# Delta net on one Trainium2 core: key norm applied to the rows of the system, query norm folded into the output norm, decay sums spread by DMA

## The chip, the cores and the metric

The kernel runs on one core of one Trainium2 chip, as one program. The metric is the device time of one launch in microseconds, the median of several runs. A core has five engines with queues of their own: TensorE (PE, with its weight loads PEld), VectorE (DVE), ScalarE (ACT), GpSimd (POOL) and SyncE (SP). All DMAs of this kernel are issued from SP's queue, in order. Each engine works through its own queue in order and waits on semaphores for the others.

## The reference

One step of a decoder layer for 1024 prompt tokens and 8 x 8 sample tokens, 1088 columns in all: a half-step SwiGLU, a mixer of two branches with a gated sum, a second half-step SwiGLU, each between RMS norms. Branch A is sliding-window attention; branch B is a short convolution and a gated delta net of 4 heads with key and value width 128. The change is within branch B:

```python
qb = l2_normalize(qb.reshape(bsz, t, B_HEADS, B_KEY_DIM)) * (B_KEY_DIM ** -0.5)
kb = l2_normalize(kb.reshape(bsz, t, B_HEADS, B_KEY_DIM))
...
gc = jnp.cumsum(g, axis=-1)
...
decay = jnp.exp(jnp.where(incl, gc[..., :, None] - gc[..., None, :], -jnp.inf))
k_beta = k * beta[..., None]
m = jnp.where(strict, jnp.einsum('...id,...jd->...ij', k_beta, k) * decay, 0.0)
a = m + jnp.eye(c, dtype=m.dtype)
...
qk = jnp.einsum('...id,...jd->...ij', q, k) * decay
q_dec = q * jnp.exp(gc)[..., None]
...
ob = rms_norm(ob, dn_out_norm) * jax.nn.silu(zb)
```

with `l2_normalize(x) = x * rsqrt(sum(x * x) + EPS)` over the 128 features of a token and head. The system `a` is solved for its right sides, a scan over chunks carries the state, and the output is normed per token and head.

## The kernel before

Tokens lie along the free dimension, features along the 128 partitions. The 1088 tokens are cut into the column blocks of 384, 384 and 320. Weights are loaded by SP in 256 KB pieces, split into two float32r parts (a high part by ACT, L111, a rest by DVE, L112), and each product is done as three (L138 to L140). The program has a first FFN, the projections for keys, values and queries of branch A with the attention, the units of the convolution (`qkv`), of z and of the gates (`ga`), four delta heads, then the branch products, the output product and the second FFN.

The framework that records the program orders the instructions on each engine. Where a delta head's small products wait, it puts products of a conv, z or gate unit (written to the tiles `pa`, three of them in PSUM) in between. DVE empties each `pa` tile (L957, L1018, L1031). The text below calls these products fillers.

`delta_head(h, A, ps)` works on eight tiles of 128 x 1088 (the set `HA` for heads 0 and 2, `YA` for 1 and 3; the profile shows all of them as `s`) and on a PSUM ring of two tiles, `ph` for heads 0 and 2, `py` for 1 and 3. Its steps:

- `l2` for q and for k (L1049, L1050). `colsum_rsqrt` squares the tile on ACT (L998), sums over the partitions by three products with a tile of ones (L1001, 512 + 512 + 64 columns), scales (L1002), takes the reciprocal root on ACT (L1003, with a table load) and refines it by a Newton step (L144 to L146). Then DVE scales the tile (L1008).
- For two groups of four chunks of 128 tokens: the running sums of g are spread over all partitions by a product of a broadcast column of g with a triangle (L1060, into `pr`), k against q (L1063), the decay (L1066, L1074, L1075), the product with it (L1077), the decay's transpose (L1080), k against k (L1083) and the system's matrix M with beta as a factor on its rows (L1087). The 64 sample tokens get the same at L1099 to L1114.
- Diagonal 32 x 32 blocks go through DRAM (`bd`) and are inverted by forward substitution on DVE (L1143, L1149), while k and v are transposed (L1135, L1202, L1203).
- The inverse is completed by products (L1174 to L1198) with the scales beta and beta exp(gc) (L1165, L1166).
- The scan over eight chunks (L1217 to L1236), then the sample tokens (L1246 to L1270).
- The output norm: `colsum_rsqrt` again, on the output tile QK (L1276), the scale (L1277), the product with z on POOL (L1278) and the store to `obd`.

The sums gc themselves, one column per chunk and head, are made once before the attention (L759 to L778).

Of the kernel before, what the change touches and what calls it, by code (L numbers as in the profile page):

```python
# [7 lines left out]
F32 = mybir.dt.float32  # L8
# [27 lines left out]
def body(ctx: ExitStack, tc: tile.TileContext, d):  # L36
# [25 lines left out]
    gd = dp.tile([16, P, NT], F32, tag="gd", name="gd")  # L62

# [716 lines left out]

    vtok = YA[6]
# [215 lines left out]
    def colsum_rsqrt(src, sq, ve, rr, tmp, scale, ps):  # L997
        nc.scalar.activation(sq, src, AF.Square)  # L998
        for a, b in ((0, 512), (512, 1024), (1024, NT)):
            pq = ps()  # L1000
            nc.tensor.matmul(pq[:, : b - a], ones, sq[:, a:b], start=True, stop=True)  # L1001
            nc.scalar.activation(ve[:, a:b], pq[:, : b - a], AF.Identity, scale=scale, bias=epsc)  # L1002
        nc.scalar.activation(rr, ve, AF.Abs_reciprocal_sqrt)  # L1003
        newton(rr, ve, tmp)

    def l2(x, A, l2s, ps):
        colsum_rsqrt(x, A[4], A[3], A[5], A[4], 0.25, ps)
        nc.vector.scalar_tensor_tensor(out=x, in0=x, scalar=-0.25 * l2s, in1=A[5], op0=ALU.mult, op1=ALU.mult)  # L1008
# [31 lines left out]
    def delta_head(h, A, ps):  # L1040
        q, k, v, M, L, U, QK, R = A
        ar = R[:, :NPR].rearrange("p (i c) -> p i c", c=P)
        mq = s2b.tile([P, 2 * NSM], F32, tag="mq", name=f"mq{h}", bufs=2)

# [4 lines left out]
        l2(q, A, P ** -0.5, ps)  # L1049
        l2(k, A, 1.0, ps)  # L1050
        def wide(t, c0):
            return t[:, c0 * P : c0 * P + 512]

        D, E = R[:, 0:512], R[:, 512:1024]
        for c0 in (0, 4):
            pr, pq = ps(), ps()
            for i in range(4):
                w, cs, ix = tile_of(c0 + i)
                ps_i = slice(i * P, i * P + P)
                nc.tensor.matmul(pr[:, ps_i], tk["g"][:, ix : ix + 1].to_broadcast([P, P]), cst[:, C_TRI : C_TRI + P], start=True, stop=True)  # L1060
            for i in range(4):
                w, cs, ix = tile_of(c0 + i)
                nc.tensor.matmul(pq[:, i * P : i * P + P], k[:, cs], q[:, cs], start=True, stop=True)  # L1063
            for i in range(4):
# [3 lines left out]
                    in0=pr[:, i * P : i * P + P],  # L1068
# [5 lines left out]
            nc.scalar.activation(E, pr, AF.Exp)  # L1074
# [6 lines left out]
            for i in range(4):  # L1081
                w, cs, ix = tile_of(c0 + i)
                nc.tensor.matmul(pk[:, i * P : i * P + P], k[:, cs], k[:, cs], start=True, stop=True)  # L1083
            nc.scalar.copy(D, pt)
            for i in range(4):
# [4 lines left out]
                    scalar=tk["beta"][:, ix : ix + 1],  # L1090
# [416 lines left out]
```

## Time and profile before

| what | value |
|---|---|
| median of 3 runs | 2460.74 us (2459.77 to 2460.8) |
| the profiled execution's own time | 2454.17 us |
| its span, first to last instruction | 2452.4 us |
| granted TensorE clock, mean | 0.991 |
| DMA traffic | 257.98 MB, 105 GB/s over the span |

The profile is of one execution, and its durations are compared with that execution's time. A page line such as `PE 2396.3 (98%) x14654` gives busy time, share of the span and instructions. A group's row has line, engine, operation, output and inputs, shape and count, then busy time and the mean of one in ns, then the idle time of the engine ahead of the group and what ended it. A wait's row reads: engine, output and line that waited, what it waited for, the time in all, how often, and the longest.

### The profile page before, as it was taken

The numbers are of one execution on the slowest core, as the hardware profiler recorded it, in microseconds if no ns is written. First come the engines' busy times: TensorE is split into PE (matmuls) and PEld (weight loads), VectorE is DVE, ScalarE is ACT, GpSimd is POOL, SyncE is SP. The second block draws the span as 40 slices with busy tenths as digits, with TensorE's granted clock in tenths as the row PEclk, the third lists the DMA queues.
The fourth block names the chain that finished last, engine by engine and source line by source line (L and its number), as shares of the span: only waits on it lengthen the run. The fifth ranks groups of instructions, "written<-read, shape, count | busy, mean of one in ns | idle before, by whom it ended". The sixth has DMA issues, their size and how long they took to land.

```text
span 2452.4 us, 39218 instructions
## 1 busy us (share of the span) xinstructions
PE 2396.3 (98%) x14654; PEld 2307.2 (94%) x14654; DVE 1752.0 (71%) x3550; ACT 1146.2 (47%) x2326; POOL 48.6 (2%) x36
## 2 busy tenths in 40 slices
PE   8999999999999999999999999999999999999997
PEld 7999999999998988798898889999999999999997
DVE  8887657757788577698796646655997576676677
ACT  7644423324465377644655333255754333233344
POOL 0000000000000000000101000000000000000000
PEclk9999999999999999999999999999999999999998
DMA  7332212213454301222222345435523122122453
GB/s 269 125 112 86 74 48 86 70 52 112 155 175 142 105 29 45 77 65 73 71 68 73 99 143 158 142 129 184 182 93 97 48 82 78 45 85 80 152 164 133
DMA packets 159759, 257.98 MB, mean 105 GB/s; under 512 B 34800, under 2 KB 65968, under 8 KB 159560
## 3 DMA queue, kind: packets, MB, share of 16 engines
q1 hardware_dynamic: 159568, 255.47, 32.4%
q8 instruction: 115, 1.88, 0.3%
q14 instruction: 76, 0.62, 0.1%
HBM read 219.43 MB, written 36.96 MB: 105 GB/s over the span
## 4 chain that ended last, share of the span: by engine, by line
PE 43%; DVE 6%; DMA 2%; ACT 1%; issue 1%; SPq 0%; DVEq 0%; ACTq 0%
PE pa L139 6%; PE pa L140 6%; PE pa L138 6%; PE pa L462 4%; PE pa L463 4%; PE pa L464 4%; PE py L344 2%; PE py L345 2%; PE ph L345 2%; PE ph L344 2%; PE ph L343 2%; PE py L343 2%; DMA q_c_a<-in_up_dram 1%; DVE s L1149 1%; DVE s L1143 1%
## 5 line engine op out<-in xcount | busy, mean ns | idle before, releaser
L463 PE MATMUL pa<-cl,h_c_s 128*128 128x384 f32 x704 | 236.4, 336 | 4.7 <-DVE cl L272 4.7
L462 PE MATMUL pa<-ch,h_c_s 128*128 128x384 f32 x704 | 237.4, 337 | 2.0 <-DVE t L468 1.4
L464 PE MATMUL pa<-ch,l_c_s 128*128 128x384 f32 x704 | 236.2, 336 | 0.0
L468 DVE TENSOR_TENSOR t<-pa,t 128x384 f32<-128x384 f32 x308 | 170.3, 554 | 83.6 <-PE pa L464 83.1
L462 PE MATMUL pa<-ch,h_c_a 128*128 128x384 f32 x528 | 176.8, 335 | 0.1
L464 PE MATMUL pa<-ch,l_c_a 128*128 128x384 f32 x528 | 176.6, 334 | 0.0
L463 PE MATMUL pa<-cl,h_c_a 128*128 128x384 f32 x528 | 176.5, 334 | 0.0
L111 ACT CAST h_c_a<-r_c_a 128x512 fp32r<-128x512 f32 x132 | 81.8, 619 | 129.8 <-PE pa L463 110.9
L462 PEld LDWEIGHTS pa<-ch,h_c_s 128*128 128x128 f32 x704 | 132.8, 189 | 5.6 <-DVE t L468 5.2
L463 PEld LDWEIGHTS pa<-cl,h_c_s 128*128 128x128 f32 x704 | 133.0, 189 | 4.9 <-DVE cl L272 4.9
L464 PEld LDWEIGHTS pa<-ch,l_c_s 128*128 128x128 f32 x704 | 132.9, 189 | 0.0
L111 ACT CAST h_c_s<-q_c_s 128x512 fp32r<-128x512 f32 x132 | 82.0, 621 | 107.1 <-PE pa L463 96.3
L139 PE MATMUL pa<-xbl,h_ga 128*128 128x384 f32 (+1 forms) x384 | 129.3, 337 | 0.0
L138 PE MATMUL pa<-xbh,h_ga 128*128 128x384 f32 (+1 forms) x384 | 128.7, 335 | 0.0
L140 PE MATMUL pa<-xbh,l_ga 128*128 128x384 f32 (+1 forms) x384 | 128.4, 334 | 0.0
L462 PEld LDWEIGHTS pa<-ch,h_c_a 128*128 128x128 f32 x528 | 99.1, 188 | 0.8 <-DVE t L468 0.6
L463 PEld LDWEIGHTS pa<-cl,h_c_a 128*128 128x128 f32 x528 | 99.1, 188 | 0.0
L464 PEld LDWEIGHTS pa<-ch,l_c_a 128*128 128x128 f32 x528 | 99.1, 188 | 0.0
L138 PE MATMUL pa<-xbh,h_qkv 128*128 128x384 f32 (+1 forms) x288 | 96.7, 336 | 0.0
L139 PE MATMUL pa<-xbl,h_qkv 128*128 128x384 f32 (+1 forms) x288 | 96.6, 335 | 0.0
L140 PE MATMUL pa<-xbh,l_qkv 128*128 128x384 f32 (+1 forms) x288 | 96.3, 334 | 0.0
L111 ACT CAST h_c_s<-r_c_s 128x512 fp32r<-128x512 f32 x44 | 27.4, 623 | 146.4 <-PE pa L463 130.6
(603 smaller groups left out, 7438.4 us busy)
## 6 DMA issues: line engine op xcount, KB each, us to landing
r_c_a<-in_up_dram SPq DMA_DIRECT2D x132, 256.0 KB
q_c_a<-in_up_dram SPq DMA_DIRECT2D x44, 256.0 KB
q_ub<-in_up_dram SPq DMA_DIRECT2D x44, 256.0 KB
r_ub<-in_up_dram SPq DMA_DIRECT2D x44, 256.0 KB
r_ua<-in_up_dram SPq DMA_DIRECT2D x42, 256.0 KB
q_ua<-in_up_dram SPq DMA_DIRECT2D x42, 256.0 KB
r_da<-in_dn_dram SPq DMA_DIRECT2D x40, 256.0 KB
q_da<-in_dn_dram SPq DMA_DIRECT2D x40, 256.0 KB
```

The costliest lines, as they stand in the source:

```text
L111: nc.scalar.copy(hi, full)
L138: nc.tensor.matmul(ps[:, :n], hi[:, j, :], at(xh, k), start=first, stop=False)
L139: nc.tensor.matmul(ps[:, :n], hi[:, j, :], at(xl, k), start=False, stop=False)
L140: mm = nc.tensor.matmul(ps[:, :n], lo[:, j, :], at(xh, k), start=False, stop=last)
L343: nc.tensor.matmul(ps[:, :n], hi[:, i, :], hh, start=i == 0, stop=False)
L344: nc.tensor.matmul(ps[:, :n], hi[:, i, :], hl, start=False, stop=False)
L345: nc.tensor.matmul(ps[:, :n], lo[:, i, :], hh, start=False, stop=i == len(hs) - 1)
L462: nc.tensor.matmul(ps, wh[:, k, :], xh[:, k, :], start=k == 0, stop=False)
L463: nc.tensor.matmul(ps, wh[:, k, :], xl[:, k, :], start=False, stop=False)
L464: nc.tensor.matmul(ps, wl[:, k, :], xh[:, k, :], start=False, stop=k == 3)
L468: nc.vector.tensor_tensor(out=out, in0=ps, in1=other, op=ALU.add)
L1143: nc.vector.tensor_tensor(out=tv, in0=Md[:, j + 1 :, j : j + 1].to_broadcast([34, m, j + 1]), in1=Ld[:, j : j + 1, 0 : j + 1].to_broadcast ...
```

## The change

Queries and keys are no longer scaled before they are multiplied. `colsum_rsqrt` and `l2` are gone.

- Keys: k is transposed at the head's start (nine transposes, which stood in the middle of the head before). ACT squares the transposed tiles, DVE reduces them to one sum per token, nine columns for a head, and a reciprocal root with a Newton step runs on these 128 x 9 values. The factors enter where beta stood: its square in the rows of M (`br2`) and in the scale of the key side (`bgr`), the factor itself on the value side (`bhr`). The old k stays as `kT_` and its tile is later reused as L; the transposed k takes the tile that was L, and the sample part has a small tile `k8`.
- Queries: the square of q, scaled with the norm's epsilon, is stored to DRAM (`sqd`) at the head's start and read back at the end, where DVE adds it to the square of the output, so that the sum over partitions under the output norm contains it. The output norm is the only one left that sums over partitions by products with ones.
- Decay sums: gc is transposed once, its 36 rows are stored to DRAM (`gcd`), and each head reads its row spread over the 128 partitions into QK by one DMA. The products L1060 and L1099 are gone; the decay and its exponents read QK in SBUF.

```diff
@@ -62,0 +63,2 @@
+    gcd = dp.tile([4, 9, P], F32, tag="gcd", name="gcd")
+    sqd = dp.tile([4, P, NT], F32, tag="sqd", name="sqd")
@@ -778,0 +781,8 @@
+    psc = pb()
+    nc.tensor.transpose(psc[:36, :P], tk["gc"], ident)
+    gct = s2b.tile([36, P], F32, tag="gct", name="gct")
+    nc.vector.tensor_copy(gct, psc[:36, :P])
+    for c in range(9):
+        nc.sync.dma_start(gcd[:, c, :], gct[4 * c : 4 * c + 4, :])
@@ -997,12 +1007,2 @@
-    def colsum_rsqrt(src, sq, ve, rr, tmp, scale, ps):
-        nc.scalar.activation(sq, src, AF.Square)
-        for a, b in ((0, 512), (512, 1024), (1024, NT)):
-            pq = ps()
-            nc.tensor.matmul(pq[:, : b - a], ones, sq[:, a:b], start=True, stop=True)
-            nc.scalar.activation(ve[:, a:b], pq[:, : b - a], AF.Identity, scale=scale, bias=epsc)
-        nc.scalar.activation(rr, ve, AF.Abs_reciprocal_sqrt)
-        newton(rr, ve, tmp)
-    def l2(x, A, l2s, ps):
-        colsum_rsqrt(x, A[4], A[3], A[5], A[4], 0.25, ps)
-        nc.vector.scalar_tensor_tensor(out=x, in0=x, scalar=-0.25 * l2s, in1=A[5], op0=ALU.mult, op1=ALU.mult)
+    eps4 = s2b.tile([P, 1], F32, tag="eps4", name="eps4")
+    nc.vector.memset(eps4, 4.0 * P * EPS * EPS)
@@ -1041 +1041,6 @@
-        q, k, v, M, L, U, QK, R = A
+        q, kT_, v, M, k, U, QK, R = A
+        L = kT_
@@ -1043,0 +1049 @@
+        k8 = s2b.tile([NSM, P], F32, tag="k8", name=f"k8{h}", bufs=2)
@@ -1049,2 +1054,0 @@
-        l2(q, A, P ** -0.5, ps)
-        l2(k, A, 1.0, ps)
@@ -1053,0 +1058,3 @@
+        nc.sync.dma_start(QK, gcd[h].rearrange("c t -> (c t)")[0:NT].unsqueeze(0).to_broadcast([P, NT]))
+        nk = s2b.tile([P, 5, 9], F32, tag="nk", name=f"nk{h}", bufs=2)
+        ss, rho, rho2, t9, bgr = (nk[:, i, :] for i in range(5))
@@ -1054,0 +1062,29 @@
+        nc.vector.memset(ss, 1.0)
+        for c0 in (0, 4, 8):
+            n = 4 if c0 < 8 else 1
+            w = P if c0 < 8 else NSM
+            pt = ps()
+            for i in range(n):
+                nc.tensor.transpose(pt[:w, i * P : i * P + P], kT_[:, (c0 + i) * P : (c0 + i) * P + w], ident)
+            nc.scalar.copy(wide(k, c0) if c0 < 8 else k8, pt[:w, : n * P])
+            nc.scalar.activation(M[:w, : n * P], pt[:w, : n * P], AF.Square)
+            nc.vector.tensor_reduce(
+                out=ss[:w, c0 : c0 + n], in_=M[:w, : n * P].rearrange("p (i c) -> p i c", c=P), op=ALU.add, axis=AX.X
+            )
+        nc.vector.tensor_scalar_add(ss, ss, 4.0 * EPS)
+        nc.scalar.activation(rho, ss, AF.Abs_reciprocal_sqrt)
+        newton(rho, ss, t9)
+        nc.vector.tensor_scalar_mul(rho, rho, -0.5)
+        nc.vector.tensor_tensor(out=rho2, in0=rho, in1=rho, op=ALU.mult)
+        def mine(nm):
+            return v94(tk[nm])[:, :, h]
+        bgr, bhr, br2 = t9, ss, bgr
+        nc.vector.tensor_tensor(out=bgr, in0=mine("bg"), in1=rho2, op=ALU.mult)
+        nc.vector.tensor_tensor(out=bhr, in0=mine("bh"), in1=rho, op=ALU.mult)
+        nc.vector.tensor_tensor(out=br2, in0=mine("beta"), in1=rho2, op=ALU.mult)
+        nc.scalar.activation(U, q, AF.Square, scale=P * EPS ** 0.5)
+        nc.sync.dma_start(sqd[h], U)
@@ -1056 +1092 @@
-            pr, pq = ps(), ps()
+            pq = ps()
@@ -1059,5 +1095 @@
-                ps_i = slice(i * P, i * P + P)
-                nc.tensor.matmul(pr[:, ps_i], tk["g"][:, ix : ix + 1].to_broadcast([P, P]), cst[:, C_TRI : C_TRI + P], start=True, stop=True)
-            for i in range(4):
-                w, cs, ix = tile_of(c0 + i)
-                nc.tensor.matmul(pq[:, i * P : i * P + P], k[:, cs], q[:, cs], start=True, stop=True)
+                nc.tensor.matmul(pq[:, i * P : i * P + P], kT_[:, cs], q[:, cs], start=True, stop=True)
@@ -1068 +1100 @@
-                    in0=pr[:, i * P : i * P + P],
+                    in0=QK[:, cs],
@@ -1074 +1106 @@
-            nc.scalar.activation(E, pr, AF.Exp)
+            nc.scalar.activation(E, wide(QK, c0), AF.Exp)
@@ -1083 +1115 @@
-                nc.tensor.matmul(pk[:, i * P : i * P + P], k[:, cs], k[:, cs], start=True, stop=True)
+                nc.tensor.matmul(pk[:, i * P : i * P + P], kT_[:, cs], kT_[:, cs], start=True, stop=True)
@@ -1090 +1122 @@
-                    scalar=tk["beta"][:, ix : ix + 1],
+                    scalar=br2[:, c0 + i : c0 + i + 1],
@@ -1097 +1129 @@
-            tri, neg = cst[:w, C_TRIS : C_TRIS + w], cst[:w, C_NEGS : C_NEGS + w]
+            neg = cst[:w, C_NEGS : C_NEGS + w]
@@ -1099,3 +1131,2 @@
-            nc.tensor.matmul(p[:, 0:w], tk["g"][:w, ix : ix + 1].to_broadcast([w, P]), tri, start=True, stop=True)
-            nc.tensor.matmul(p[:w, 128 : 128 + w], k[:, cs], k[:, cs], start=True, stop=True)
-            nc.tensor.matmul(p[:w, 256 : 256 + w], k[:, cs], q[:, cs], start=True, stop=True)
+            nc.tensor.matmul(p[:w, 128 : 128 + w], kT_[:, cs], kT_[:, cs], start=True, stop=True)
+            nc.tensor.matmul(p[:w, 256 : 256 + w], kT_[:, cs], q[:, cs], start=True, stop=True)
@@ -1104 +1135 @@
-                out=Ds, in0=p[:w, 0:w], scalar=tk["gc"][:w, ix : ix + 1], in1=neg, op0=ALU.subtract, op1=ALU.add
+                out=Ds, in0=QK[:w, cs], scalar=tk["gc"][:w, ix : ix + 1], in1=neg, op0=ALU.subtract, op1=ALU.add
@@ -1108 +1139 @@
-            nc.scalar.activation(eR, p[:, 0:w], AF.Exp)
+            nc.scalar.activation(eR, QK[:, cs], AF.Exp)
@@ -1115 +1146 @@
-                out=M[:w, cs], in0=p[:w, 128 : 128 + w], scalar=tk["beta"][:w, ix : ix + 1], in1=DT, op0=ALU.mult, op1=ALU.mult
+                out=M[:w, cs], in0=p[:w, 128 : 128 + w], scalar=br2[:w, c : c + 1], in1=DT, op0=ALU.mult, op1=ALU.mult
@@ -1132,5 +1163,4 @@
-            for t in (k, v):
-                p = ps()
-                for i in range(4):
-                    nc.tensor.transpose(p[:, i * P : i * P + P], t[:, (c0 + i) * P : (c0 + i + 1) * P], ident)
-                nc.scalar.copy(wide(t, c0), p)
+            p = ps()
+            for i in range(4):
+                nc.tensor.transpose(p[:, i * P : i * P + P], v[:, (c0 + i) * P : (c0 + i + 1) * P], ident)
+            nc.scalar.copy(wide(v, c0), p)
@@ -1165,2 +1195,2 @@
-            nc.vector.tensor_scalar_mul(Ub, U[:w, cs], tk["bg"][:w, ix : ix + 1])
-            nc.scalar.mul(U[:w, cs], U[:w, cs], tk["bh"][:w, ix : ix + 1])
+            nc.vector.tensor_scalar_mul(Ub, U[:w, cs], bgr[:w, c : c + 1])
+            nc.scalar.mul(U[:w, cs], U[:w, cs], bhr[:w, c : c + 1])
@@ -1202 +1231,0 @@
-        nc.tensor.transpose(p[:w, 0:128], k[:, cs], ident)
@@ -1204 +1233 @@
-        nc.scalar.copy(ar[:w, 6:8, :], p[:w, 0:256].rearrange("p (i c) -> p i c", c=P))
+        nc.scalar.copy(ar[:w, 7, :], p[:w, 128:256])
@@ -1208 +1237 @@
-        nc.tensor.matmul(p5[:, :w], ar[:w, 6, :], Ub, start=True, stop=True)
+        nc.tensor.matmul(p5[:, :w], k8, Ub, start=True, stop=True)
@@ -1269 +1298 @@
-            nc.tensor.matmul(p6, ar[:NSM, 6, :], vm, start=True, stop=True)
+            nc.tensor.matmul(p6, k8, vm, start=True, stop=True)
@@ -1276 +1305,9 @@
-        colsum_rsqrt(QK, q, k, v, M, 1.0 / P, ps)
+        nc.sync.dma_start(v, sqd[h])
+        nc.scalar.activation(q, QK, AF.Square)
+        nc.vector.tensor_tensor(out=q, in0=q, in1=v, op=ALU.add)
+        for a, b in ((0, 512), (512, 1024), (1024, NT)):
+            pq = ps()
+            nc.tensor.matmul(pq[:, : b - a], ones, q[:, a:b], start=True, stop=True)
+            nc.scalar.activation(k[:, a:b], pq[:, : b - a], AF.Identity, scale=1.0 / P, bias=eps4)
+        nc.scalar.activation(v, k, AF.Abs_reciprocal_sqrt)
+        newton(v, k, M)
```

The changed instructions stand in a different order on the engines. Three places follow. In the rows `s_...` are a head's wide tiles, `pa_...` the fillers' output, `eye_72` holds the identity and the ones; line numbers of the first fence of a pair are those of the kernel before, those of the second of the changed kernel.

TensorE at the start of the third head (its ring is `ph`, while the second head's scan L1217 to L1235 runs on `py`), before: the products with ones for k's norm (L1001) and behind them the first spread of the sums of g (L1060).

```order
L1001 MATMUL ph_12686<-s_8312,eye_72 128x512
L1001 MATMUL ph_12689<-s_8312,eye_72 128x512
L1224 MATMUL py_11724<-s_8307,s_8303 128x128
L1235 MATMUL py_11731<-s_8306,s_8307 128x128
L1001 MATMUL ph_12692<-s_8312,eye_72 128x64
L140 MATMUL pa_13257<-xbh_1_8036,l_ga_1_13225 128x384
L138 MATMUL pa_13257<-xbh_1_8036,h_ga_1_13224 128x384
L1060 MATMUL ph_12700<-cst,tk_g 128x128
L1217 MATMUL py_11735<-s_8304,s_8301 128x128
L1219 MATMUL py_11735<-s_8307,s_8305 128x128
L1234 MATMUL py_11742<-s_8302,s_8307 128x128
L1060 MATMUL ph_12700<-cst,tk_g 128x128 x3
```

The same place in the changed kernel: the last transposes of k (L1068) and k against q (L1095), with the second head's inverse (L1204 and on, before L1174 and on) between them.

```order
L140 MATMUL pa_13159<-xbh_0_8245,h_ga_0_13091 128x320
L1068 MATMUL ph_12669<-eye_72,s_8311 128x128 x2
L1068 MATMUL ph_12677<-eye_72,s_8311 64x128
L141 MATMUL pa_13159<-xbl_0_8247,h_ga_0_13091 128x320
L1204 MATMUL py_11605<-s_8303,s_8307 128x128 x4
L142 MATMUL pa_13159<-xbh_0_8245,l_ga_0_13092 128x320
L1095 MATMUL ph_12694<-s_8310,s_8311 128x128 x4
L1208 MATMUL py_11611<-s_8309,s_8305 128x128 x4
```

The products with ones and the spread of g are gone, transposes of k stand at the start of the head, and k against q follows them with no spread of g ahead of it. The third head now starts beside the second head's inverse and not beside its scan.

TensorE at the output norm of the second head, before: the two products for the new sample states (L1269), one filler, and the products with ones (L1001), with transposes of the next head (L1135) between them.

```order
L1269 MATMUL py_11821<-s_8303,s_8307 128x512
L1269 MATMUL py_11825<-s_8303,s_8307 128x512
L140 MATMUL pa_13327<-xbh_0_7313,l_qkv_0_13318 128x384
L1001 MATMUL py_11831<-s_8302,eye_72 128x512
L1135 MATMUL ph_12786<-eye_72,s_8309 128x128
L1001 MATMUL py_11834<-s_8302,eye_72 128x512
L1001 MATMUL py_11837<-s_8302,eye_72 128x64
```

The same place in the changed kernel, from the second product for the sample states (L1298) to the first with ones (L1310):

```order
L1298 MATMUL py_11810<-s_8302,k_11402 128x512
L141 MATMUL pa_13258<-xbl_1_8248,h_ga_1_13196 128x320
L142 MATMUL pa_13258<-xbh_1_8246,l_ga_1_13197 128x320
L140 MATMUL pa_13299<-xbh_0_7315,h_qkv_0_13289 128x384
L141 MATMUL pa_13299<-xbl_0_7317,h_qkv_0_13289 128x384
L142 MATMUL pa_13299<-xbh_0_7315,l_qkv_0_13290 128x384
L140 MATMUL pa_13299<-xbh_0_7315,h_qkv_0_13289 128x384
L1310 MATMUL py_11818<-s_8304,eye_72 128x512
```

Six fillers stand there now, and three more stand between the two L1298.

DVE at the same output norm in the changed kernel: the sum that closes the output (L1285), the masks (L1291), the two additions to the sample states (L1299) and the new addition of sqd (L1307), with the release of a filler's tile (L1031).

```order
L1285 TENSOR_TENSOR s_8308<-py_11798,s_8309 128x64
L1291 TENSOR_TENSOR s_8302<-s_8309,cst 64x512
L1299 TENSOR_TENSOR s_8305<-s_8305,py_11806 128x512
L1307 TENSOR_TENSOR s_8304<-s_8304,s_8306 128x1088
L1031 SCALAR_TENSOR_TENSOR t_1142_13283<-pa_13258,r_8267 128x320
L114 TENSOR_TENSOR l_ga_1_14143<-r_ga_1_14140,h_ga_1_14142 128x512
L1299 TENSOR_TENSOR s_8305<-s_8305,py_11810 128x512
```

The new addition stands ahead of a filler's release and of the second L1299.

## The prediction

> **What bounds the kernel now.** I read the head of the page first, then the windows of the stage that the change touches, then the waits of TensorE there, and last single stretches of its timeline.
>
> ```profile
> span 2452.4 us, 39218 instructions
> PE 2396.3 (98%) x14654; PEld 2307.2 (94%) x14654; DVE 1752.0 (71%) x3550; ACT 1146.2 (47%) x2326; POOL 48.6 (2%) x36
> 900.00:1460.00 560.00, 544.14 (x3522) 483.97 (x3523) 413.66 (x1090) 301.97 (x670) 48.42 (x32) 0.99 0.24 74
> 1460.00:1640.00 180.00, 180.00 (x1110) 179.39 (x1109) 110.16 (x206) 67.75 (x139) 0.00 (x0) 1.00 0.48 155
> ```
>
> In a window's row the columns are its bounds, its length, the busy time of PE, weight loads, DVE, ACT and POOL, the granted clock, the DMA share and GB/s. TensorE is busy 98% of the span. The four delta heads run from about 900 to 1460 us, and there TensorE is busy 544 of 560 us, because the products of the conv, z and gate units are woven between the heads' own small products. After the last head comes a stretch of 180 us without a gap, gate products and then the branch products. So no head's chain sets the end: the length of the stage is **the sum of TensorE's work, plus its gaps, plus what a lowered clock costs**. A microsecond of TensorE work taken out of the stage shortens the kernel by a microsecond, as long as no new gap takes its place; DVE (414 of 560) and ACT (302) have room.
>
> **What TensorE loses and gains.** Three lines lose work. The first is L1001, the sums of squares over the partitions by a product with ones. It has three calls per head, for q, k and the output; q's and k's go.
>
> ```profile
> 900.00:1460.00 560.00, 28.32 (x72) 12.18 (x72) 0.99 0.24 74
> 900.00:1460.00 560.00, 9.57 (x64) 8.29 (x64) 0.99 0.24 74
> 900.00:1460.00 560.00, 1.98 (x8) 1.38 (x8) 0.99 0.24 74
> 1351.12 2.23 PE L1001 MATMUL ph<-s,eye 128*128 128x512 f32 x6
> 1353.16 0.42 PE L138 MATMUL pa<-xbh,h_ga 128*128 128x384 f32 x1
> 1353.42 0.33 PE L139 MATMUL pa<-xbl,h_ga 128*128 128x384 f32 x1
> 1353.59 0.33 PE L140 MATMUL pa<-xbh,l_ga 128*128 128x384 f32 x1
> 1005.92 0.94 PE L1060 MATMUL ph<-cst,tk_g 128*128 128x128 f32 x6
> 1006.61 0.42 PE L139 MATMUL pa<-xbl,h_qkv 128*128 128x384 f32 x1
> ```
>
> The first three rows are PE and PEld busy time of L1001, L1060 and L1099 alone, over the four heads. Each float32 product shows as two records: L1001's 72 are 36 products, 3 per call. Matmuls overlap at their ends, so I price by start to start. A call of L1001 (6 records) starts at 1351.12 and the next product at 1353.16: 2.04 us. Eight calls go: 8 x 2.04 = **16.3 us**. L1060, the running sums of g spread over the partitions, goes entirely: six records take 1006.61 - 1005.92 = 0.69 us, so 0.115 each, and 64 x 0.115 = **7.4 us**. L1099, the same for the sample rows, has 8 records of half the width; at no more than 0.115 each **0.9 us**. Together 24.6 us. The upper bound is busy time, which counts overlapped ends too: 28.32 x 2/3 + 9.57 + 1.98 = 30.4 us. A part of that extra is real: after a float32 group the next filler products start 0.26 us apart and not 0.17 (1353.16, 1353.42, 1353.59).
>
> Added is one transpose of gc ahead of the attention, two records: 0.2 us. The nine transposes of k per head (eight at L1135, one at L1202) move to the head's start, at the same count. Net **-24.4 us**.
>
> **What changes on the other engines.** Before, per head:
>
> ```profile
> L145 DVE TENSOR_TENSOR s<-s,s 128x1088 f32<-128x1088 f32 x12 | 15.4, 1280 | 3.6 <-ACT s L144 3.6
> L146 DVE SCALAR_TENSOR_TENSOR s<-s,s 128x1088 f32<-128x1088 f32 x12 | 15.4, 1283 | 0.1
> L1008 DVE SCALAR_TENSOR_TENSOR s<-s,s 128x1088 f32<-128x1088 f32 x8 | 10.2, 1281 | 0.0
> L804 DVE TENSOR_REDUCE st<-s 128x4 f32<-128x1024 f32 x10 | 12.2, 1217 | 0.1
> L998 ACT ACTIVATE s<-s 128x1088 f32<-128x1088 f32 x12 | 13.3, 1108 | 11.0 <-DVE s L1256 5.7 <-DVE s L146 3.2 <-issue 2.1
> ```
>
> DVE loses two of each of L145, L146 and L1008 per head, 6 x 1.28 = 7.7 us. It gains one full-width addition (1.28, the price of L145), two reductions of 512 elements and one of 128 (half of L804's 1.22 us each, and a little: 1.4), and nine operations on 9 columns (estimated at under 0.2 us each: 1.6). Net about -3.4 us per head. ACT loses two wide squares (1.1 each), their scalings, roots and second squares, and gains a wide square of q and small ones. Neither engine sets the end, so I count **nothing**; what hides it is the fillers, and if they ran out DVE's difference would count in favour of the change too. The second exponent now reads QK in SBUF and no longer waits for a product.
>
> **DMA.** SP issues nine small DMAs for gcd, and per head three of 544 KB: QK from gcd, sqd out, sqd back. An issue occupies SP for a third of a microsecond, 21 in all, 7 us in the shadow of a queue that already waits much longer without starving TensorE:
>
> ```profile
> SPq L1033 <- ACT t L1032: 75.8, 29, 11.1
> SPq L126 <- DVE t L960: 18.3, 2, 16.8
> 984.75 0.33 SPq L901 DMA_DIRECT2D s<-in_kc_dram  x1
> 988.53 0.17 PEld L910 LDWEIGHTS py<-s,qs 64*32 64x32 f32 x8 [0.38 <-DMA s<-in_kc_dram]
> 1145.87 1.95 PE L1246 MATMUL ph<-mq,s 128*128 128x16 f32 x16
> 1149.82 0.43 PE L1255 MATMUL ph<-s,s 64*128 64x64 f32 x2
> DVE s L1143 <- DMA s<-bd: 1.2, 2, 0.8
> ```
>
> No spread of one row over 128 partitions stands in the trace of before. Its nearest row is the load of kc (512 KB, behind vc's): issued at 984.75, and the product that waits for it starts at 988.53, so 3.8 us. At the least it is hidden altogether. At the most, only head 0 is exposed: its QK buffer is free only when the attention's last products are done, and the first subtraction (L1066) then stands on DVE 3.8 us later; queued behind it are the releases of the tiles pa, of which there are three, each worth 24 products of 0.17 us, 4.1 us. So a wait of 3.8 us empties about one tile of three. I take **0** and keep 4 us for the range. The other heads' DMAs are issued earlier against their use. The new wait of sqd's way back stands at the output norm: the addition (DVE) waits for it, and behind the addition are an L1270 and again the releases of pa. v is free from the head's last L1217, and from the sample products (L1246, 1145.87 in head 0) to the one whose result closes the output (L1255, 1149.82) pass 4.0 us, then the square (1.1 us); that is longer than the 3.8 us, so I take 0 here too.
>
> The output norm's chain on TensorE gets longer by that addition, 1.28 us. The order of the new program puts 8 to 13 more fillers around and behind the two state products (L1269 before): at least 8 x 0.17 = 1.4 us. I count 0, with -1 to +2 us per head in the range.
>
> **Gaps and clock.** These were TensorE's waits in the stage that hang on lines which go or change, and the half-rate stretches:
>
> ```profile
> PE py L1001 <- ACT s L998: 2.2, 2, 1.8
> PE py L1001 <- ACT s L1002: 1.3, 1, 1.3
> PE ph L1080 <- ACT s L1075: 1.4, 1, 1.4
> PE ph L1083 <- DVE s L1077: 1.1, 1, 1.1
> PE ph L1001 <- ACT s L998: 0.7, 1, 0.7
> PE ph L1063 <- DVE s L1008: 0.6, 1, 0.6
> 1024.00:1026.00 2.00, 0.59 (x5) 0.40 (x5) 2.00 (x5) 1.12 (x2) 0.87 (x1) 1.00 0.33 66
> 1028.00:1030.00 2.00, 2.00 (x11) 1.66 (x10) 1.55 (x6) 1.61 (x2) 0.00 (x0) 0.50 0.00 0
> 1032.00:1034.00 2.00, 2.00 (x6) 1.48 (x5) 0.24 (x1) 0.00 (x0) 0.00 (x0) 0.50 0.24 37
> 1178.00:1180.00 2.00, 2.00 (x8) 2.00 (x7) 1.46 (x10) 1.97 (x3) 0.00 (x0) 0.51 0.00 0
> 1348.00:1350.00 2.00, 2.00 (x6) 0.98 (x5) 0.66 (x4) 0.71 (x1) 0.00 (x0) 0.83 0.08 29
> ```
>
> The waits of L1001 and L1063 for q's and k's norm are 1.8 + 1.3 + 0.7 + 0.6 = 4.4 us. They go. L1080 and L1083 in head 0 (2.5 us together) ran with no filler between them and the products ahead; the new order puts eight and fifteen fillers ahead of the two groups of L1080. After gaps the granted clock falls to half: from 1028 to 1034 us (3 us lost) and near 1178 (1 us and some). So up to 6.9 + 4 = 11 us could go. But the new products wait as well: k's transposes for the conv, M's release for the new chain reduction, root, scale (L1087). I take a quarter of the 11 as the net: **-3 us**, from 0 to -11, and above zero, +8 us, if the new places gap like head 0's did.
>
> **Sum.** On the profiled execution's own time, 2454.17 (span 2452.4 and 1.8 around it): 2454.2 - 24.4 - 3 = 2426.8, so -27.4 us or 1.1%. The runs' median, 2460.74, lies 6.6 us above that execution; 2460.7 - 27.4 = **2433.3 us**.
>
> **Rivals.**
> *Half clock at the transposes.* The new heads begin with nine transposes of k and DVE-bound waits where dense products with ones stood. If each head then lost what head 0 lost before, 3 us of clock (1028 to 1034), 4 x 3 = 12 us come back, and no gap goes: 2460.7 - 24.4 + 12 = 2448. For it: three half-rate stretches in the trace. Against it: 1028 followed 2.5 us of gaps within 4 us, and fillers now stand around the transposes. [...]
>
> ```profile
> 1036.43 1.04 PE L1135 MATMUL ph<-eye,s 128*128 128x128 f32 x8
> 1036.00:1038.00 2.00, 2.00 (x15) 1.78 (x14) 2.00 (x3) 2.00 (x6) 0.99 (x1) 1.00 0.03 4
> ```
>
> Chance 0.12.
> *Nothing gained.* If the end hung on the heads' chains, removed products would turn into gaps: 2460. Against it stand the 180 us without a gap behind the last head. That the removed products stay in the program can be left out, since their rows are gone from TensorE's order. 0.05.
> *Slower: the addition at the output norm waits for sqd.* The place is DVE's queue in each head. If the way back is issued late (SP was seen to wait 16.8 us at one DMA) DVE stands still, three pa tiles cover 3 x 4.1 = 12 us at the most, and then TensorE stops. It decides against the change from 24.4 / 4 = 6.1 us of TensorE per head, so from a wait of some 18 us in every head; at 20 us, 8 us per head: 2460.7 - 24.4 + 32 = 2468. The longest wait of DVE for a DMA in this stage was 0.8 us (L1143, shown with the DMAs). 0.04.
>
> **How the numbers follow.** The forecast, gain of 15 to 38 us, has 0.79. The low end is the upper bound of the products, 30.4 - 0.2, with 8 of the 11 us of gaps: 2422. The high end takes 24.4 with both +8 of gaps and +4 of the broadcast, 2448, which just takes in the first rival's time. Outside I leave about 0.2: the two last rivals, and the tails of the first and of the forecast. This kernel's runs tell 0.2%, 4.9 us, from no change. Faster by more: 0.91; within: 0.05; slower: 0.04.
>
> **What would show it.** PE's busy time in the heads' stage falls by 24 us or more at unchanged fillers, and the stage from 900 us to the end of the gates shortens by as much; the product with ones is left with 24 records, one call per head, and the transposes of k keep 72 at 0.115 us each. DVE's busy time falls by some 14 us. Right on the gaps: TensorE's waits in the stage stay under 16 us and no more than three stretches have half the clock. Wrong: DVE waiting on gcd or sqd with TensorE idle behind it, or half-rate stretches at each head's start.

## The result, and the profile after

| | before | changed |
|---|---|---|
| median of the runs side by side | 2460.26 us (2457.51 to 2460.8, 4 runs) | 2438.76 us (2437.43 to 2445.16, 4 runs) |
| all runs of the study | 2458.9 us (median of 74) | 2438.8 us (median of 9) |
| profiled execution, span, mean clock | 2454.17, 2452.4, 0.991 | 2439.36, 2437.6, 0.990 |

The ratio is 0.992 (95% interval 0.9901 to 0.9939): 20 us faster, where 27.4 were forecast. The forecast time, 2433.3 us, was 5.5 us too low, and the range held the result.

The head of the changed kernel's page, then its windows: bounds, length, busy time of PE, weight loads, DVE, ACT and POOL, granted clock, DMA share and GB/s. The last two rows are PE and weight loads alone: first of L1310 (the one product with ones that is left), then of L1068 (the transposes of k).

```profile
span 2437.6 us, 39030 instructions
PE 2377.6 (98%) x14535; PEld 2295.3 (94%) x14535; DVE 1734.6 (71%) x3580; ACT 1110.8 (46%) x2298; POOL 50.2 (2%) x36
900.00:1440.00 540.00, 520.03 (x3378) 464.84 (x3377) 390.43 (x1103) 266.11 (x645) 50.03 (x32) 0.98 0.28 88
1440.00:1625.00 185.00, 185.00 (x1139) 184.39 (x1139) 112.02 (x209) 69.67 (x143) 0.00 (x0) 1.00 0.47 151
900.00:1440.00 540.00, 8.99 (x24) 4.19 (x24) 0.98 0.28 88
900.00:1440.00 540.00, 6.00 (x36) 3.97 (x36) 0.98 0.28 88
```

The stage is still bounded by TensorE, and behind the last head there is again a stretch without a gap (185 of 185 us). PE is busy 18.7 us less over the span (2396.3 to 2377.6). But in the stage it now idles 20 of 540 us, where it idled 16 of 560. Its waits there (output and line that waited, what for, time in all, how often, longest):

```profile
PE py L1112 <- ACT s L1107: 3.9, 1, 3.9
PE pa L140 <- DVE t L975: 2.6, 1, 2.6
PE py L1204 <- DMA s<-bd: 2.3, 1, 2.3
PE py L1068 <- DVE s L1173: 1.9, 1, 1.9
PE ph L875 <- ACT s L824: 1.9, 5, 0.7
PE py L929 <- ACT s L824: 1.6, 2, 0.8
PE py L1068 <- DVE s L1003: 1.5, 2, 1.0
```

The waits of L1001 and L1063 for the norm of q and k are gone. In their place TensorE waits for the decay's exponent (L1107), for k as the convolution delivers it (L1003) and for two tiles that VectorE empties late (L140).

For all comparisons below I split the stage, from the first product of a qkv unit to the last of a ga unit, from the trace's starts of TensorE's instructions: work is start to start at full clock, gap is time between a modelled end and the next start, and clock is what half rate added. For the two profiles:

| in the stage, us | before | changed | difference |
|---|---|---|---|
| length | 632.9 | 619.6 | -13.3 |
| work: the heads' small products | 205.4 | 179.9 | -25.5 |
| work: the 2303 fillers (qkv, z, ga) | 403.4 | 409.0 | +5.6 |
| gaps | 17.3 | 21.1 | +3.8 |
| lowered clock | 6.8 | 9.6 | +2.8 |

The last row does not carry over to the runs. Every run lists its span and mean granted clock, and their product is the span at full clock: on average 2434.4 us before (74 runs) and 2415.5 changed (9 runs), so -18.9, and the rest, lost to a lower clock, is 22.9 and 22.2. Work and gaps of the stage account for 16.1 of the 18.9 us; where the other 2.8 us went, no trace here shows.

### The profile page after: what moved, and what is told of

It is laid out like the page before. It is cut to its first block, busy times and chain, and to the rows that moved or that the text cites. A ratio compares the mean times of both kernels' runs of the same rounds, so it can differ in the third digit from the quotient of the medians.

```text
span 2437.6 us, 39030 instructions
## 1 busy us (share of the span) xinstructions
PE 2377.6 (98%) x14535; PEld 2295.3 (94%) x14535; DVE 1734.6 (71%) x3580; ACT 1110.8 (46%) x2298; POOL 50.2 (2%) x36
## 4 chain that ended last, share of the span: by engine, by line
PE 45%; DVE 4%; DMA 1%; ACT 1%; issue 1%; POOL 0%; SPq 0%; DVEq 0%; ACTq 0%
PE pa L141 6%; PE pa L140 6%; PE pa L142 6%; PE pa L464 4%; PE pa L465 4%; PE pa L466 4%; PE ph L346 2%; PE ph L347 2%; PE py L347 2%; PE py L346 2%; PE py L345 2%; PE ph L345 2%; DVE s L1173 0%; DVE s L1179 0%; DMA q_db<-in_dn_dram 0%
## 5 line engine op out<-in xcount | busy, mean ns | idle before, releaser
L140 PE MATMUL pa<-xbh,h_ga 128*128 128x384 f32 (+1 forms) x384 | 129.7, 338 | 3.5 <-DVE t L975 2.6
L140 PE MATMUL pa<-xbh,h_qkv 128*128 128x384 f32 (+1 forms) x288 | 97.5, 339 | 0.0
L113 ACT CAST h_c_s<-r_c_s 128x512 fp32r<-128x512 f32 x44 | 27.4, 622 | 148.1 <-PE pa L465 134.1
```

The costliest lines, as they stand in the source:

```text
L113: nc.scalar.copy(hi, full)
L140: nc.tensor.matmul(ps[:, :n], hi[:, j, :], at(xh, k), start=first, stop=False)
```

## Experiments

Twelve runs were made, two of them of the old and the changed kernel again. They fall into three questions: what each part is worth, who makes the gaps, and how good one profile is as a base.

### The kernels again

> The changed kernel as it is, on the chip of the runs beside it, as their base. If the time is TensorE's work plus gaps plus half-rate stretches, 2438.8 us again within 4 us either way, the scatter going with the mean granted clock: 0.001 of clock is about 2.4 us. If the change's first runs were lucky, 2445 us or more.

Measured: 2438.82 us (2437.55 to 2440.41, 5 runs), and in its profile work 589.6, gaps 21.0, clock 8.0. Held.

> The kernel before once more, for a second profile of it. Its first profile (execution 2454.17 us) had 17.3 us of TensorE gaps and 6.8 us of lowered clock in the stage of the delta heads; its timed median is 2458 to 2460. If that profile was of a quick execution, this one, near the median, has the same TensorE work in the stage (608.8 within 1 us) and 4 to 6 us more in gaps and lowered clock together. Rival: the work itself differs from one execution to the next by over 2 us.

Measured: its profiled execution took 2453.84 us, again a quick one, its 8 runs 2455.99 in the median (ratio 0.9989, 0.9972 to 1.0007). Work 609.2 and gaps 17.2 repeat to 0.4 us; clock was 3.5 and not 6.8. So the work holds from one execution to the next, and so did the stage's gaps in these two pairs of profiles. No profile of a median execution of before came up, and what its other 5 us are was not seen in a trace; over the 74 runs the spans were 2449.0 to 2466.4 us, the shortest at a clock of 0.996, the longest at 0.986.

### What the parts are worth

First the six products with ones per head were put back with nothing that reads them, TensorE's work without a chain:

```diff
+        for dead in (q, kT_):
+            for a, b in ((0, 512), (512, 1024), (1024, NT)):
+                pd = ps()
+                nc.tensor.matmul(pd[:, : b - a], ones, dead[:, a:b], start=True, stop=True)
```

> The changed kernel with the six products with ones per head put back as products alone, of q and of k as they are; nothing reads their results. If TensorE's work sets the time, they cost what the trace of before gave them, 16.3 to 17 us, so 2455 us. If the stage is set by the heads' chains, on which these products do not lie, they fill gaps: under 8 us, 2447 or less.

Measured: 2448.03 us (2443.21 to 2450.57, 10 runs), ratio 0.9957 (0.9939 to 0.9976): +9.2 us. At full clock the mean span rose by 12.3 us, in the profile the work by 14.0 (small products +14.9) with gaps 3.2 lower; the mean loss to the clock fell by 4.3. Neither size was met: **TensorE's work counts, but in this run the gaps and the clock's loss were smaller as well**, and some 5 us of the 14 came back that way. Whether that is due to the dense products themselves or to the new order of the instructions, this one run does not tell.

Then each part was undone in the changed kernel, the rest left as it is. Keys: `l2(kT_, A, 1.0, ps)` and the transposes of before, with the plain factors beta, bg and bh. Queries: `l2(q, A, P ** -0.5, ps)`, no sqd, the old output norm. Sums: L1060 and L1099 of before, no gcd.

> The changed kernel with the keys' part undone: k is normed by products with ones and transposed in the middle of the head, as before. By TensorE's work: 8.4 us of products with ones come back and some 12 interruptions of the fillers go (0.13 us each, 1.6), so +6.9 us, 2445.7. If the new chain of reduction, root and scale on the rows is what makes TensorE wait (3.9 us at the transpose of the decay in head 1, and the half-rate stretch behind it), these waits go as well and the time stays within 2 us of the changed kernel's.

> The changed kernel with the queries' part undone: q normed by products with ones at the head's start, no store and reload of its square, the output norm over the output alone. By TensorE's work +8.4 us, 2447. If the reload and the longer output norm cost waits, less than +5 us; if q's norm also delays k against q, more than +11.

> The decay sums by products of TensorE again (L1060, L1099 of before), the rest as in the changed kernel. Theory A, the price of a part is its TensorE work: the products put back took 7.4 and 0.9 us, so 2438.8 + 8 = 2447. Theory B, from the keys' and the queries' part, each of which cost 22 us to undo where its work was 5 to 7: any other order of the work costs 10 to 15 us more in gaps and lowered clock, so about 2455 to 2460. Rival: hidden, 2439.

Measured: 2461.15 (2458.3 to 2466.51, 10 runs), 2460.4 (2457.18 to 2464.22, 10 runs) and 2446.01 us (2440.26 to 2449.22, 5 runs). The sums cost what their work is, within that scatter. The keys or the queries undone cost the whole gain, each alone. For the keys both theories were wrong by 15 us or more. For the queries the work alone was wrong by 13 us; of the conditions beside it, "more than +11" if q's norm delays k against q was met with +21.6. But in that profile the norm's own products (L1010) wait 4.0 us for ScalarE and k against q (L1107) 1.7, while 9.8 us of the 21.6 are a lower clock (32.0 lost for 22.2), so that delay is a part at most. Since three such prices (22, 22 and 7) can't add up to 20, the other half of the combinations was run: each part alone on the kernel before.

> The keys' part alone on the kernel before (queries scaled as before, decay sums by products). Undoing the queries' part gave 2460.4, undoing the decay sums' part cost 7.2. Theory A, the parts add up but for the two norms, which pay only together: 2460.4 + 7 = 2467. Theory B, the work counts and the waits of the kernel with the queries undone came from the decay sums spread by DMA (its exponents start at once and stand ahead of the wide norm on ScalarE): 2459 less the keys' work of about 7 = 2452.

> The queries' part alone on the kernel before. Theory A: 2461.2 + 7 = 2468. Theory B: 2459 less the queries' work of about 5 = 2454.

> The decay sums' part alone on the kernel before: TensorE's work in the stage down by 8. Theory A, the parts add up: 2459 - 7 = 2452. Theory B, beside a wide norm the spread sums bring waits: 2456 to 2465.

All eight combinations; the first columns are runs, the last four the profile of each in the stage (for all parts and for none, two profiles). The last column sums TensorE's waits for ACT from 850 to 1470 us.

| parts in | median us | ratio to before | span at full clock | lost to the clock | work | gaps | clock | waits for ACT |
|---|---|---|---|---|---|---|---|---|
| none | 2458.9 | 1 | 2434.4 | 22.9 | 608.8, 609.2 | 17.3, 17.2 | 6.8, 3.5 | 8.9 |
| keys | 2463.73 | 1.0026 (1.0009 to 1.0043) | 2432.8 | 29.3 | 601.1 | 25.1 | 12.5 | 11.4 |
| queries | 2451.25 | 0.9971 (0.9957 to 0.9985) | 2428.4 | 22.1 | 603.7 | 18.0 | 9.7 | 7.5 |
| sums | 2465.39 | 1.003 (1.0013 to 1.0047) | 2435.6 | 27.8 | 602.6 | 28.5 | 9.7 | 17.8 |
| keys, queries | 2446.01 | 0.9942 (0.992 to 0.9965) | 2418.6 | 23.9 | 594.1 | 17.1 | 6.7 | 3.0 |
| keys, sums | 2460.4 | 1.0006 (0.9989 to 1.0023) | 2426.7 | 32.0 | 594.0 | 26.2 | 18.2 | 17.5 |
| queries, sums | 2461.15 | 1.001 (0.9991 to 1.0029) | 2429.1 | 30.8 | 596.6 | 27.9 | 15.3 | 12.7 |
| all | 2438.8 | 0.9925 (0.99 to 0.995) | 2415.5 | 22.2 | 588.9, 589.6 | 21.1, 21.0 | 9.6, 8.0 | 9.6 |

What the reader is to see: **the work adds up and the time does not.** Against 609.0, the mean of none, keys take 7.9 us of work, queries 5.3, sums 6.4, together 19.6; all three measured 19.4 to 20.1, and the three pairs lie 0.7 to 1.7 us above their sums. But the sums alone make the kernel slower (6 us, interval clear of 1), and so do the keys alone; the time they lose is in gaps (+11.2 and +7.9) and in the clock. The queries alone gain 7.7 us, more than their work. Keys and queries together gain 13, about their work, and have no more gaps than before. The framework ordered each of these kernels anew, so a part and the order that comes with it were not separated, and why one order has more gaps than another stays open.

Of the six expectations the sums undone met theory A; the queries alone are nearest to theory B (2451 for 2454); the keys alone lie between the two; the sums alone rose as theory B said (2465.4 for 2456 to 2465). The last column shows that the sums add waits for ACT in each of the four pairs of rows, 8.9, 6.1, 5.2 and 6.6 us. But theory B's idea was that they do so beside a wide norm, and the last pair has none of q's and k's wide norms. The waits of TensorE with the sums alone, where both wide norms stand (L1007 squares and L1011 scales for them, L1081 is the decay's exponent, L823 the attention's):

```profile
PE py L1010 <- ACT s L1007: 3.1, 2, 2.4
PE py L1010 <- ACT s L1011: 3.0, 1, 3.0
PE ph L874 <- ACT s L823: 2.7, 7, 0.7
PE ph L1086 <- ACT s L1081: 2.6, 1, 2.6
PE py L928 <- ACT s L823: 2.4, 1, 2.4
```

And with keys and queries but without the sums, the two rows for ACT of over 0.5 us:

```profile
PE ph L866 <- ACT s L815: 1.6, 4, 0.6
PE po L876 <- ACT s L871: 1.2, 3, 0.5
```

In the first the late ones are the wide norms' own steps as much as the exponents. Are exponents ahead of them in ScalarE's queue? ScalarE's timeline ahead of the two longest waits at L1010 (2.43 us up to 1070.79, 2.99 up to 1279.15) says no:

```profile
1068.16 0.52 ACT L1029 ACTIVATE t<-t 128x384 f32<-128x384 f32 x1 [2.85 <-DVE s L1002]
1069.63 1.11 ACT L1007 ACTIVATE s<-s 128x1088 f32<-128x1088 f32 x1 [0.95 <-DVE s L147]
1278.00 0.52 ACT L1001 ACTIVATE t<-t 128x384 f32<-128x384 f32 x1 [2.89 <-DVE t L974]
1278.43 1.51 ACT L1011 ACTIVATE s<-py,epsc 128x512 f32<-128x512 f32 x3
```

No exponent stands in the 9 us ahead of either. ScalarE itself sat idle for 2.85 and 0.95 us ahead of the first and 2.89 us ahead of the second, until VectorE had finished. So at these two waits VectorE is the late engine, and ACT, the name in the last column, is only the last step. How the spread sums bring the other waits stays open.

### Who makes the gaps

The longest wait of the changed kernel stands in the second head, at L1112. ScalarE's timeline ahead of it:

```profile
1055.35 0.63 ACT L1106 ACTIVATE s<-s 128x512 f32<-128x512 f32 x1 [1.80 <-POOL s L1108]
1056.00 1.28 ACT L1075 ACT_TABLE_LOAD   x1
1057.29 0.21 ACT L1075 ACTIVATE nk<-nk 128x9 f32<-128x9 f32 x1
1057.52 1.28 ACT L1107 ACT_TABLE_LOAD   x1
1058.81 0.63 ACT L1107 ACTIVATE s<-s 128x512 f32<-128x512 f32 x1
```

A root of 9 columns, 0.21 us, stands between two exponents with two table loads of 1.28 us around it, 2.8 us in all, and TensorE waits 3.9 us. So the exponents were ordered behind the root, within ScalarE's queue:

```diff
-        nc.scalar.activation(rho, ss, AF.Abs_reciprocal_sqrt)
+        root = nc.scalar.activation(rho, ss, AF.Abs_reciprocal_sqrt)
...
-            nc.scalar.activation(E, wide(QK, c0), AF.Exp)
-            nc.scalar.activation(D, D, AF.Exp)
+            for ex in (nc.scalar.activation(E, wide(QK, c0), AF.Exp), nc.scalar.activation(D, D, AF.Exp)):
+                tc.add_manual_dep(ex.ins, root.ins.name, NOSYNC, reason="exponents behind the root")
```

> The changed kernel with the exponents of a head (L1106, L1107) held behind that head's small root (L1075) in ScalarE's order. It adds no wait between engines, only an order within one. If the wait of 3.9 us at L1112 in head 1 comes from the two table loads of 1.28 us around the small root, it goes, and with it the stretch at half clock behind it (1.7 us): 2433 to 2436. Rival: the root is held by DVE's sums (L1068 and what follows), the exponents come later instead, and the time stays at 2438.8 or rises by the same 2 to 5 us.

Measured: 2439.64 us (2438.03 to 2446.63, 4 runs), ratio 0.9926 (0.9899 to 0.9953): no gain. At that place ScalarE now loads tables once on either side of the root, ahead of all exponents (1.28 us each, from 1051.07 and from 1052.59 us). So the two loads were moved and not removed, the product waits all the same, and then the next one waits for VectorE. TensorE at the same place and at the start of the third head:

```profile
1055.19 1.03 PE L1112 MATMUL py<-eye,s 128*128 128x128 f32 x4 [2.88 <-ACT s L1106]
1058.10 2.07 PE L1115 MATMUL py<-s 128*128 128x128 f32 x8 [1.87 <-DVE s L1109]
1156.65 0.52 PE L1068 MATMUL ph<-eye,s 128*128 128x128 f32 x3 [3.84 <-DVE s L1003]
```

The first theory fell: 3.9 us at one place became 2.9 + 1.9 there, and 3.8 us came up at a place that had no such wait, while the 2.6 us at L140 close to it went. The rival (same time) held. What a kernel without the two loads would gain was not run.

The second longest wait stands at L140 near 1155.5 us: a filler waits for a tile `pa` that VectorE should have emptied (L985 reads it; the profile names L975, which ends at the same time). VectorE and GpSimd ahead of it:

```profile
1149.16 4.32 POOL L1315 TENSOR_TENSOR s<-s,s 128x1088 f32<-128x1088 f32 x1 [19.86 <-DVE s L1179]
1150.99 2.90 DVE L975 SCALAR_TENSOR_TENSOR t<-t,vec,t 128x384 f32<-128x384 f32 x1
1153.42 1.00 POOL L1184 MEMSET s<- 128x1088 f32 x1
1153.82 1.57 DVE L970 COPY t<-ncv 128x3 f32<-128x3 f32 x1
1153.89 1.50 DVE L985 SCALAR_TENSOR_TENSOR t<-pa,r 128x64 f32<-128x64 f32 x1
1154.02 1.36 DVE L975 SCALAR_TENSOR_TENSOR t<-t,vec,t 128x384 f32<-128x384 f32 x1
1154.36 1.00 POOL L1185 MEMSET s<- 128x1088 f32 x1
1155.44 0.56 DVE L967 SCALAR_TENSOR_TENSOR t<-pa,r 128x384 f32<-128x384 f32 x1
1155.53 0.60 PE L140 MATMUL pa<-xbh,h_ga 128*128 128x384 f32 x1 [2.62 <-DVE t L975]
```

L975 takes 0.61 us elsewhere and here 2.90. A copy of three columns (L970, 0.16 us elsewhere) takes 1.57 and ends at 1155.39, as GpSimd's second fill does (1155.36); L985 and L975 behind it end there too. Over the stage 16 VectorE instructions that overlap one of GpSimd's last over 0.3 us longer than the median of their line, tiles and shape, 20 us in all (the expectation below says 23 and 32, which the trace does not give); before it was 8 and 13 us. Of those that overlap none, not one is stretched by that much. The longest is an L114 of 2.98 us, for 0.69 elsewhere, and each stretched instruction ends with GpSimd's or up to 0.8 us behind it.

So GpSimd's seven operations went to VectorE (`nc.gpsimd.tensor_tensor` and `nc.gpsimd.memset` became `nc.vector...` in L1108, L1140, L1160, L1184, L1185, L1286 and L1315), in the changed kernel and in the one with the keys undone.

> The changed kernel with all seven wide operations of GpSimd (L1108, L1140, L1160, L1184, L1185, L1286, L1315) on VectorE. In the profile of the changed kernel 23 VectorE instructions that overlap one of them last 32 us longer than others of their form in all, and several end with GpSimd's. Theory A, those operations hold VectorE up and so hold back evictions: the waits of TensorE for VectorE in the stage (2.6 at L140, 0.9, 1.9, 0.9) shrink by 3 to 5 us, with 2 to 4 us of lowered clock: 2431 to 2435, and no VectorE instruction is stretched by over 0.3 us. Rival: VectorE, 80 per cent busy from 900 to 1320 us, gets some 30 us more of work and becomes late itself: 2440 to 2450.

> The changed kernel with the keys' part undone, as in the earlier run (2461.2), and GpSimd's seven operations on VectorE. In that run three of TensorE's waits (2.75, 2.58, 3.47 us, for evictions of VectorE) stand at a VectorE instruction that lasts until a GpSimd operation ends, and a stretch of 3.41 us at half clock follows each. Theory: these are what the kernel pays above its work, 8.8 us of waits and 5.1 us of clock, so 2461 - 14 = 2447. Rival: as in the changed kernel without GpSimd (2436.6 against 2438.8), VectorE is late at other places instead: 2456 to 2461.

Measured: 2436.64 us (2435.73 to 2440.35, 4 runs), ratio 0.9913 (0.9886 to 0.994), in the changed kernel, 2.2 us lower than with GpSimd, with intervals that overlap, and between theory A (2431 to 2435) and its rival (2440 to 2450); 2449.81 us (2445.51 to 2452.78, 9 runs), ratio 0.9962 (0.9947 to 0.9977), with the keys undone, 11.3 us lower and clear of it. In the first GpSimd is busy for 0.00 us from 900 to 1440 us, so no VectorE instruction there overlaps one of its any more. But the gaps did not go: 21.0 us in the first, as with GpSimd, and 24.2 for 27.9 in the second. VectorE itself is late now, at other places: in the first, TensorE's waits for VectorE rise from 8.9 to 15.8 us, and those for ScalarE fall from 9.5 to 4.4. The changed kernel without GpSimd:

```profile
PE pa L140 <- DVE t L1018: 7.2, 4, 3.1
PE pa L140 <- DVE t L1031: 5.0, 1, 5.0
PE pa L140 <- DVE t L967: 2.7, 1, 2.7
```

What went is the clock's loss, in the stage's profile 9.6 to 5.8 us and 15.3 to 5.5, in the means of the runs 22.2 to 20.1 and 30.8 to 23.1. With the keys undone the theory (2447) is nearer than its rival (2456 to 2461), but by the clock and 4.4 us at full clock, not by the 8.8 us of waits that it named.

Without GpSimd is the quickest version of this study; 2.2 us beside a scatter of 8 us is not told apart from the changed kernel.

### Where the clock falls

In the changed kernel three stretches of half clock begin where a wait of over 2 us ends: 1060.0 us (behind L1112's 3.89), 1155.6 (behind L140's 2.62), 1367.2 (behind L1204's 2.31). Others follow no gap at all. TensorE's timeline in the first head, and two windows:

```profile
1125.13 0.33 PE L141 MATMUL pa<-xbl,h_qkv 128*128 128x384 f32 x1
1125.30 1.96 PE L1275 MATMUL ph<-mq,s 128*128 128x16 f32 x16
1127.19 0.43 PE L1276 MATMUL ph<-s,s 64*128 64x64 f32 x2
1128.62 0.53 PE L140 MATMUL pa<-xbh,h_qkv 128*128 128x384 f32 x1
1128.00:1130.00 2.00, 2.00 (x9) 1.85 (x8) 1.17 (x3) 0.26 (x1) 1.29 (x1) 0.57 0.59 170
1155.60:1158.00 2.40, 2.40 (x8) 2.40 (x9) 2.40 (x5) 0.73 (x2) 0.00 (x0) 0.50 0.41 81
```

L1275 is sixteen records of 16 columns (0.26 us each), each with a weight load of 128x128 (0.19 us); PE counts as busy, and one microsecond behind it the fillers run at half rate (0.53 us in place of 0.33). In the 14 profiles of this study, from 845 to 1640 us, half clock stood within 3.5 us of the end of 36 of 45 waits of 2 us and more, of 12 of 45 between 1 and 2 us and of 1 of 45 between 0.7 and 1 us (waits close together share a stretch); 19 stretches had no such wait, and 17 of them began right behind these sample products. The sample products run 56 times in the 14 profiles, and 20 times a stretch began within 3.5 us of them, so they too are followed by half clock, less often than long waits. No run changed them, so this is a pattern and not an experiment. In the profiles of before and after, ahead of the last 16 us of the span, 13 stretches lasted 3.41 us (eight) or 6.83 us (five) at a clock of 0.50, so each costs up to half its length: the six of the changed kernel's stage, 20.5 us together, cost 9.6.

## Why the prediction was right, and where its sizes were off

- **What bounds the stage: right.** Work adds up to 0.5 us of 20 for the three parts and to 1.7 us for the pairs, and put back without a chain it cost 9.2 us. That time follows work to the microsecond was too simple: it held for the sums undone (+7.2 for 5 to 6) and failed for keys or queries undone. So that the whole change came out inside the range is luck in part: keys and sums take 15.0 us of work out and gained nothing (ratio 1.0006), queries and sums 12.4 and nothing (1.001), and the same way of adding up would have missed these by 12 us or more.
- **Products removed, -24.6 + 0.2: right.** Start to start, L1001's 24.0 us became 7.1 at L1310, so -16.9 for 16.3; L1060 -7.2 for 7.4; L1099 -1.3 for 0.9. The sum of these, -25.4, is 0.8 us off.
- **The fillers were left out: a term put at nothing that was 5.6 us.** The prediction saw that the first filler behind a small product takes 0.26 and not 0.17 us and counted that as a possible gain. It went the other way: the same 2303 fillers took 5.6 us more, because the small products cut them into 191 runs where there were 173. From start to start a filler takes 0.165 us within a run, 0.26 as the first of one and 0.22 as the last, so an interruption costs about 0.15 us; 18 more and somewhat dearer edges make about 4 of the 5.6 us, the rest is spread thinly over the others. The 14 profiles bear it out: the same fillers take from 403.5 us in 173 runs to about 409 in 191, and a line through all 14 rises by 0.21 us for each run more. The work term was -20, not -24.4.
- **Gaps and clock, -3: wrong in sign.** The 4.4 us of waits for q's and k's norm went, but new ones came at L1112, L1068 and L140, +3.8 us net in the stage. The clock gave about nothing (22.9 to 22.2 in the means). Together it is 3 us instead of -3, 6 us off and as large a miss as the fillers, within the bound of +8 that the text gave.
- **From the profile to the median.** Worked on the profiled executions alone the change is worth 14.8 us, on medians 20. Adding 6.6 us to a profiled execution was right: it had been quicker than the median, as the second one was. But the gain forecast, 27.4, missed the profiled executions by 12.6 us and the medians by 7.4. The 5 us between them stand in no trace, so the smaller miss is luck in part too.
- **VectorE: right in size** (1752.0 to 1734.6, -17.4 for -14) and in worth: nothing that shows. The nine operations on 9 columns, put at under 0.2 us each, took 0.07 to 0.17 us in the changed kernel, but for L1078 (0.44 in the mean, 1.25 once beside one of GpSimd's). **DMA: right.** VectorE waited 0.6 us for gcd (L1098), and for sqd at L1307 not at all, so the slower rival had no place.
- **Half clock at the transposes: did not come.** No stretch begins behind L1068 alone. The six of the stage begin at 1060.0, 1155.6 and 1367.2 us behind the waits named above, at 1128.3 and 1210.2 behind the sample products (L1275), and at 855.2 behind the narrow products of the sums of g (L763 to L768, 2.0 us for outputs of 4 to 32 columns). In the kernel before, eight records of transposes alone (L1135, from 1036.43 us) ran at a clock of 1.00.
- **What would show it:** met by L1310's 24 records and VectorE; not met by PE's busy time (-18.7 over the span for -24), by the waits under 16 us (the rows of the whole answer sum to 20.8) and by three stretches of half clock (six). k's transposes are 36 records and not the 72 given, which had v's with them. And the stated gain of 15 to 38 us does not fit the stated bounds: the high end, 2448, is a gain of 12 to 13.

## What to carry to other kernels

Where TensorE bounded the stage (busy 520 of 540 us), the work that the change removed added up, to 0.5 us of 20, and could be priced row by row; but price the woven work beside it too, since each new interruption of it cost 0.15 us here. Don't judge the parts of a change by undoing one at a time alone: here two of the three, put in alone, made the kernel slower, and two of them, undone alone, each seemed to be worth everything. A wait that was taken away at one place came back at the next here (21.0 to 21.6 us of gaps in three versions of this kernel, with VectorE busy 387 to 399 and ScalarE 266 to 270 of 540 us), and 36 of 45 waits of 2 us and more were followed by half clock, which costs up to 1.7 us for each 3.41 us that it lasts.

## What the runs showed of the hardware

Half clock lasted 3.41 or 6.83 us at a time (13 stretches in the profiles of before and after) and stood mostly behind TensorE's waits of 2 us and more (36 of 45), and sometimes behind thin dense products (16 columns, 1.9 us; 20 of 56). VectorE's operations took up to 2.98 us, where they take 0.69 elsewhere (L114), beside one of GpSimd's wide ones: a copy of three columns took 1.57 us for 0.16, and moving 50 us of GpSimd's work to VectorE raised VectorE's busy time by only 8 us (1734.6 to 1742.5) and lowered the clock's loss by 2 and by 8 us. Two table loads around a root of 9 columns cost 2.6 us of ScalarE, and ordering them ahead of the exponents gained nothing.
